# Inverse square roots by GpSimd's power with one Newton step, and a convolution's first tap on ScalarE, in a hybrid encoder layer

## The chip, the cores and the metric

The kernel runs on one core of a Trainium2 chip. The core has five engines, each with its own instruction queue worked off in order: TensorE (PE, with PEld for its weight loads), VectorE (DVE), ScalarE (ACT), GpSimd (POOL) and SyncE (SP, which here only issues DMAs). They meet through semaphores. The metric is the device time of one execution in microseconds; a kernel's time is the median of its runs.

## The reference

One layer of an encoder: 2048 tokens, 1024 channels, three head groups that read the same normalised input, an output projection, then a gated MLP with a causal depthwise convolution, and a last normalisation. Cut to what the change touches:

```python
def rmsnorm(x, g):
    r = lax.rsqrt(jnp.mean(xf * xf, axis=-1, keepdims=True) + EPS)
    return (xf * r * g).astype(x.dtype)

# x -> h = rmsnorm(x): input projection
#   A: S5 state-space layer + GLU
#   B: differential attention, 6 heads; o = rmsnorm(o, subln_g) per head
#   C: HGRN2 recurrence, 6 heads;       o = rmsnorm(o, norm_g) per head
# x = x + concat(A, B, C) @ w_out;      h = rmsnorm(x)

def conv_glu_ffn(h, w_up, w_gate, conv_w, conv_b, w_down):
    up = h @ w_up
    gate = h @ w_gate
    up = causal_depthwise_conv(up, conv_w, width=3) + conv_b
    return (jax.nn.gelu(up) * gate) @ w_down
# x = x + conv_glu_ffn(h); out = rmsnorm(x)
```

## The kernel before

All large products are float16 triples: each operand is split into a high half and a low half, and three products are summed (`three`, line 93). A split (`split`, line 51) is an ACT copy that makes the high half and a subtraction on DVE (lines 60 and 62) or POOL (line 58) that makes the low one. The feed-forward products are further cut by a seven-product scheme of sums of quarters: seven products per 128 channels, with their sums on DVE and POOL (`add`, line 1836; tiles `f_k`, `f_u`).

Stages, in the order of time of the profiled execution:

- 0 to 500 us: the input is normalised (`norm`, line 206) and projected, and head group A runs beside it.
- 500 to 1160 us: attention for the first eight query blocks (`phase_attn`) is woven with head group C (`phase_hgrn`). Per query block and head: scores on PE (tile `t_ps`, line 834), a biased copy with running maximum on DVE (`t_sc`, `t_mx`, line 838), the exponential on ACT (line 850), a join of the two maps on DVE (line 869), the split on ACT (line 892) and POOL (line 893), a transposing DMA, and the product with the values on PE (`t_po`, line 915).
- 1160 to 1300 us: the output projection of the first half of the tokens, its normalisation (`scaled`, line 1509) and the transposes that feed the MLP.
- 1300 to 1860 us: the up and gate products with their convolution for the first half (`activations`, `tile_of`: 22 channel tiles), woven with attention for the last eight query blocks.
- 1860 to 2190 us: the down product of the first half, the output projection of the second.
- 2190 to 2590 us: up and gate products of the second half; 2590 to 2794 us: its down product, with the last normalisation (`finish`, line 1593).

What is woven is decided by generators with weights, and a scheduler then sets each engine's queue by its own timeline of the whole program. So a changed instruction in one place can shift rows on every engine behind it.

`Ctx.rsqrt` (line 66) makes an inverse square root of a [128, n] tile v wholly on DVE: a shift (line 72) and an integer form (line 75) give a guess `y` (tile `rs_y`), then three Newton steps, each of lines 81, 86 and 87 (tile `rs_t`); for n = 1 line 79 makes -v/2 once and line 86 falls away. So 11 DVE instructions for n > 1 and 9 for n = 1. It is called 48 times:

| caller | tile v | n | calls |
|---|---|---|---|
| `norm` of the input | `a_v` | 4 | 4 |
| `fin` of head group C | `g_ss` | 8 | 12 |
| `norm` of an attention head | `t_e` | 8 | 12 |
| `scaled` | `o_v` | 4 | 4 |
| `finish` | `f_v` | 1 | 16 |

`conv` (line 1608) runs once per channel tile and token half, 44 times: the first tap (line 1609) scales `u` into `t0` (tile `f_t`) by a channel's weight, two further taps (line 1613) add to it, all three on DVE over 128x1024 float32. ACT's GELU (line 1884) reads the sum, then DVE multiplies it with the gate (line 1888).

Of the kernel before, what the change touches and what calls it, by code (L numbers as in the profile page):

```python
# [9 lines left out]
F32 = mybir.dt.float32  # L10
F16 = mybir.dt.float16
I32 = mybir.dt.int32
U8 = mybir.dt.uint8
AF = mybir.ActivationFunctionType
ALU = mybir.AluOpType
# [24 lines left out]
class Ctx:  # L40


    def __init__(self, tc, const):
        self.tc = tc
        self.nc = nc = tc.nc
        self.ident = const.tile([128, 128], F32, name="ident")
        make_identity(nc, self.ident)
        self.pairs = []
        self.pace = 1.0

# [15 lines left out]
    def rsqrt(self, pool, v, n, tag):  # L66

        nc = self.nc
        i = pool.tile([128, n], I32, tag=tag + "i", name="rs_i")
        y = pool.tile([128, n], F32, tag=tag + "y", name="rs_y")  # L70
        t = pool.tile([128, n], F32, tag=tag + "t", name="rs_t")
        nc.vector.tensor_scalar(
            out=i, in0=v.bitcast(I32), scalar1=1, scalar2=None, op0=ALU.logical_shift_right
        )
        nc.vector.tensor_scalar(
            out=y.bitcast(I32), in0=i, scalar1=-1.0, scalar2=float(0x5F3759DF), op0=ALU.mult, op1=ALU.add
        )
        if n == 1:
            nc.vector.tensor_scalar(out=i.bitcast(F32), in0=v, scalar1=-0.5, scalar2=None, op0=ALU.mult)
        for _ in range(3):  # L80
            nc.vector.scalar_tensor_tensor(
                out=t, in0=y, scalar=i.bitcast(F32)[:, 0:1] if n == 1 else -0.5, in1=y,
                op0=ALU.mult, op1=ALU.mult,
            )
            if n > 1:
                nc.vector.tensor_tensor(out=t, in0=t, in1=v, op=ALU.mult)
            nc.vector.scalar_tensor_tensor(
                out=y, in0=t, scalar=1.5, in1=y, op0=ALU.add, op1=ALU.mult
            )
        return y  # L90
# [1330 lines left out]
def phase_tail(K, x, Xd, Yd, Ad, w_out, norm_g, W, conv_w, conv_b, w_down, final_g, out, es,  # L1421
# [5 lines left out]
    tc, nc = K.tc, K.nc  # L1427
    V = nc.vector
# [15 lines left out]
    cw = cp.tile([128, 3, MF], F32, name="f_cw")  # L1444
# [161 lines left out]
            nc.sync.dma_start(out=out[0, r0:r0 + 128, cc], in_=r[:, cc])  # L1606

    def conv(u, t0, m, n):
        V.tensor_scalar(
            out=t0, in0=u[:, 0:n], scalar1=cw[:, 0, m:m + 1], scalar2=None, op0=ALU.mult  # L1610
        )
        for c in (1, 2):
            V.scalar_tensor_tensor(  # L1613
                out=t0, in0=u[:, c:n + c], scalar=cw[:, c, m:m + 1], in1=t0,
                op0=ALU.mult, op1=ALU.add,
            )
# [222 lines left out]
    def tile_of(hc, m, st, sm, wp, tp, pm, few, done, new):  # L1839
# [16 lines left out]
        def room(i, bufs=None):  # L1856
# [24 lines left out]
        nc.scalar.copy(halo[:, m, :], u[:, N:])  # L1881
        t0 = tp.tile([128, N], F32, tag="t0", bufs=few + 1, name="f_t0")
        conv(u, t0, m, N)
        nc.scalar.activation(
            out=t0, in_=t0, func=AF.Gelu_apprx_tanh, bias=cb[:, m:m + 1], scale=IWS
# [232 lines left out]
```

## Time and profile before

| what | before |
|---|---|
| median of 3 runs | 2815.44 us (2808.53 to 2818.59) |
| the profiled execution, its own time | 2795.69 us |
| its span | 2794.0 us |
| busy: PE, DVE, ACT, POOL | 2442.0, 2004.2, 1222.2, 1309.4 us |
| instructions on DVE, ACT, POOL | 3893, 2231, 1095 |
| mean granted TensorE clock | 0.93 |

Busy time is summed over the whole span, while the stages differ: an engine that is busy 72% of the span, as DVE is, can be the one that is waited for in some stages and of no account in others. A row of a group of instructions reads: source line, engine, operation, output tile, input tiles, shapes, count, busy time in us, mean duration in ns, then the idle time of that engine just ahead of these instructions and what ended it.

### The profile page before, as it was taken

The page shows a single profiled execution, that of the slowest core. Times are in us where ns is not written, and L with a number is a line of the kernel's source. Part 1 is how long each engine was busy: PE and PEld are TensorE (multiplying, and loading weights), DVE is VectorE, ACT ScalarE, POOL GpSimd, SP SyncE. Part 2 cuts the span into 40 slices and gives each one's busy share as a digit, 9 for nine tenths or more (in the row PEclk, how much of TensorE's full clock was granted, in tenths as well). Part 3 has the DMA queues.
Part 4 walks back from the last instruction along what each step waited for, and adds up shares of the span by engine and source line. Part 5 has one row for each costly group of instructions (what it writes and reads, how often), then busy time and mean ns, then how long its engine had stood idle before and what let it go on. Part 6 is the DMA issues. An engine that isn't in the chain of part 4 may idle for free. (4 is left out here: it accounts for less than half of the span.)

```text
span 2794.0 us, 42749 instructions
## 1 busy us (share of the span) xinstructions
PE 2442.0 (87%) x15438; PEld 1375.0 (49%) x15438; DVE 2004.2 (72%) x3893; ACT 1222.2 (44%) x2231; POOL 1309.4 (47%) x1095
## 2 busy tenths in 40 slices
PE   5998897989988888677998887859899999999998
PEld 3654546867766764243443333324344444444443
DVE  7466746789988897688779899975654855555575
ACT  5333344556645663565345555552234422222221
POOL 4788602334334432246666666631802344444180
PEclk8999998989989988788999999979999999999999
DMA  6675554555464656864455655587775655554733
GB/s 226 232 219 192 162 174 101 123 131 132 90 150 98 132 130 134 253 171 120 164 172 158 175 140 159 142 256 239 258 268 192 221 164 154 166 155 143 270 103 121
DMA packets 554533, 474.13 MB, mean 170 GB/s; under 512 B 276880, under 2 KB 432848, under 8 KB 553296
## 3 DMA queue, kind: packets, MB, share of 16 engines
q1 hardware_dynamic: 532144, 431.02, 54.1%
q10 hardware_dynamic: 22176, 40.38, 4.0%
q8 instruction: 121, 1.98, 0.3%
q14 instruction: 92, 0.75, 0.1%
HBM read 289.30 MB, written 127.93 MB: 149 GB/s over the span
## 5 line engine op out<-in xcount | busy, mean ns | idle before, releaser
L98 PE MATMUL f_pm<-f_q,f_w 128*128 128x512 f16 x3696 | 841.3, 387 | 37.9 <-DVE f_u L1837 21.7
L98 PEld LDWEIGHTS <-f_w 128*128 128x128 f16 x3696 | 363.7, 99 | 506.7 <-issue 90.4
L1772 PE MATMUL f_pd<-f_dw,f_da 128*128 128x512 f16 x1848 | 406.5, 383 | 11.7 <-DVE f_r L1750 10.4
L893 POOL TENSOR_TENSOR t_sc<-t_sc 128x1024 f16<-128x1024 f32 (+7 forms) x144 | 250.2, 1749 | 338.9 <-ACT t_sc L892 313.5
L1772 PEld LDWEIGHTS <-f_da 128*128 128x128 f16 x1848 | 181.8, 99 | 233.0 <-issue 18.5
L850 ACT ACTIVATE t_sc<-t_sc,t_nm 128x128 f32<-128x128 f32 (+7 forms) x192 | 229.1, 1195 | 99.1 <-DVE t_nm L845 91.7
L834 PE MATMUL t_ps<-t_k,t_q 96*128 96x512 f16 (+2 forms) x480 | 168.7, 377 | 99.0 <-DVE t_mx L838 86.6
L838 DVE CUSTOM_DVE_ANT_0 t_sc<-t_ps,t_base,t_mx 128x512 f32<-128x512 f32 (+3 forms) x288 | 185.1, 643 | 28.2 <-PE t_ps L834 21.5
L60 DVE TENSOR_TENSOR f_a<-f_t,f_a 128x512 f16<-128x512 f32 x132 | 148.1, 1129 | 46.1 <-ACT f_a L54 42.0
L98 PE MATMUL g_pq<-g_h,g_w 128*128 128x256 f16 x1152 | 158.6, 298 | 16.7 <-DVE g_sg L1162 10.6
L915 PE MATMUL t_po<-t_v,t_wt 128*128 128x64 f16 x2448 | 123.2, 201 | 56.4 <-DMA t_wt<-t_sc 48.7
L915 PEld LDWEIGHTS <-t_wt 128*128 128x128 f16 x2448 | 109.2, 104 | 123.1 <-DMA t_wt<-t_sc 67.0
L1837 POOL TENSOR_TENSOR f_t<-f_t,f_t 128x512 f32<-128x512 f32 x66 | 106.8, 1632 | 129.3 <-ACT f_a L54 108.3
L1487 PE MATMUL o_pm<-o_w,o_y 128*128 128x512 f16 x624 | 147.1, 394 | 19.9 <-DMA o_y<-Yd 14.1
L869 DVE SCALAR_TENSOR_TENSOR t_sc<-t_sc,t_a 128x1024 f32<-128x1024 f32 (+7 forms) x144 | 163.2, 1159 | 0.9
L1837 POOL TENSOR_TENSOR f_k<-f_k,f_k 128x512 f32<-128x512 f32 x88 | 124.7, 1417 | 73.2 <-ACT f_k L1869 68.3
L98 PE MATMUL g_pv<-g_w,g_h 128*128 128x256 f16 x1152 | 151.5, 288 | 8.0 <-ACT g_w L54 4.7
L62 DVE SCALAR_TENSOR_TENSOR f_dw<-f_db,f_dw 128x1536 f16<-128x1536 f32 (+1 forms) x36 | 104.1, 2910 | 73.8 <-ACT f_dw L54 73.7
L1837 POOL TENSOR_TENSOR f_db<-f_db 128x1536 f32<-128x1536 f32 (+1 forms) x32 | 128.2, 4044 | 60.6 <-DMA f_db<-in_w_down_dram 60.6
L892 ACT CAST t_sc<-t_sc 128x1024 f16<-128x1024 f32 (+7 forms) x144 | 112.1, 793 | 93.1 <-DVE t_sc L869 89.5
L54 ACT ACTIVATE f_w<-f_sum 128x512 f16<-128x512 f32 x110 | 69.2, 629 | 182.4 <-DVE f_sum L141 76.9
L54 ACT ACTIVATE f_a<-f_t 128x512 f16<-128x512 f32 x154 | 95.5, 628 | 114.5 <-POOL f_t L1837 56.6
(327 smaller groups left out, 4534.8 us busy)
## 6 DMA issues: line engine op xcount, KB each, us to landing
f_w<-Wd SPq DMA_DIRECT2D x231, 256.0 KB, 3.0
Wd<-f_w SPq DMA_DIRECT2D x154, 256.0 KB, 2.1
Ad<-f_a ACTq DMA_DIRECT2D x154, 256.0 KB, 2.8
f_da<-Ad SPq DMA_DIRECT2D x42, 768.0 KB, 4.4
g_h<-Hd SPq DMA_DIRECT2D x24, 1024.0 KB, 7.0
f_db<-in_w_down_dram SPq DMA_DIRECT2D x24, 768.0 KB, 10.5
o_wst<-in_w_out_dram SPq DMA_DIRECT2D x32, 512.0 KB, 5.4
o_y<-Yd SPq DMA_DIRECT2D x52, 256.0 KB, 4.7
```

Source lines behind the costliest of these rows:

```text
L54: nc.scalar.activation(out=hi, in_=src, func=AF.Copy, scale=scale)
L60: nc.vector.tensor_tensor(out=lo, in0=src, in1=hi, op=ALU.subtract)
L98: nc.tensor.matmul(out=out, lhsT=lhs(a, k), rhs=rhs(b, k), start=(n == 0), stop=(n == 3 * nk - 1))
L834: nc.tensor.matmul(out=ps[:, 0:k1 - k0], lhsT=qt[:, c, 128 * (i % 4):128 * (i % 4) + 128], rhs=H.k[:, c, k0:k1], start=True, stop=True,)
L838: V.tensor_tensor_reduce(out=sc[c][:, k0:k1], in0=ps[:, 0:k1 - k0], in1=bs[:, k0:k1], scale=1.0, scalar=-3e38 if j == 0 else mx[:, c, j - ...
L850: nc.scalar.activation(out=sc[c][:, 0:L], in_=sc[c][:, 0:L], func=AF.Exp, scale=SLOPES[h], bias=nm[:, c:c + 1], accum_out=H.la[:, c, n_:n_ ...
L869: V.scalar_tensor_tensor(out=sc[0][:, k0:k1], in0=sc[1][:, k0:k1], scalar=a[:, 1:2], in1=sc[0][:, k0:k1], op0=ALU.mult, op1=ALU.add,)
L893: nc.gpsimd.tensor_tensor(out=hl[:, LM + k0:LM + k1], in0=sc[0][:, k0:k1], in1=hl[:, k0:k1], op=ALU.subtract,)
L915: nc.tensor.matmul(out=po, lhsT=wt[:, w, b, :], rhs=vt[:, b, 64 * v:64 * v + 64], start=(b == 0 and w + v == 0), stop=(b == i and w == 1),)
L1487: nc.tensor.matmul(out=ps[t], lhsT=y[:, k, a, 128 * t:128 * t + 128], rhs=w[:, b, k, :], start=(q == qs[0] and i == 0), stop=(q == qs[-1] ...
L1772: nc.tensor.matmul(out=ps[t], lhsT=a[:, q, x, tk], rhs=w[:, y, q, :], start=(first and q + x + y == 0), stop=(last and q == n - 1 and y == 1),
L1837: eng.tensor_tensor(out=o, in0=a, in1=b, op=op)
```

## The change

Two edits. `rsqrt` starts from GpSimd's `tensor_tensor` with the power operation: y = v to the power of a constant -0.5, read with stride 0 from a [128, 1] tile `mhalf`; one Newton step on DVE follows. The guess, its tile `rs_i` and two of the three Newton steps go. For n = 1 the one step is written as three instructions. In `conv` the first tap becomes an ACT copy with the weight as its per-partition scale.

```diff
+        self.mhalf = const.tile([128, 1], F32, name="mhalf")
+        nc.gpsimd.memset(self.mhalf, -0.5)
...
     def rsqrt(self, pool, v, n, tag):
-        i = pool.tile([128, n], I32, tag=tag + "i", name="rs_i")
         y = pool.tile([128, n], F32, tag=tag + "y", name="rs_y")
         t = pool.tile([128, n], F32, tag=tag + "t", name="rs_t")
-        nc.vector.tensor_scalar(
-            out=i, in0=v.bitcast(I32), scalar1=1, scalar2=None, op0=ALU.logical_shift_right
-        )
-        nc.vector.tensor_scalar(
-            out=y.bitcast(I32), in0=i, scalar1=-1.0, scalar2=float(0x5F3759DF), op0=ALU.mult, op1=ALU.add
-        )
-        if n == 1:
-            nc.vector.tensor_scalar(out=i.bitcast(F32), in0=v, scalar1=-0.5, scalar2=None, op0=ALU.mult)
-        for _ in range(3):
-            nc.vector.scalar_tensor_tensor(
-                out=t, in0=y, scalar=i.bitcast(F32)[:, 0:1] if n == 1 else -0.5, in1=y,
-                op0=ALU.mult, op1=ALU.mult,
-            )
-            if n > 1:
-                nc.vector.tensor_tensor(out=t, in0=t, in1=v, op=ALU.mult)
+        nc.gpsimd.tensor_tensor(
+            out=y, in0=v, in1=self.mhalf.to_broadcast([128, n]), op=ALU.pow
+        )
+        nc.vector.scalar_tensor_tensor(
+            out=t, in0=y, scalar=v[:, 0:1] if n == 1 else -0.5, in1=y, op0=ALU.mult, op1=ALU.mult
+        )
+        if n == 1:
+            nc.vector.tensor_scalar(
+                out=t, in0=t, scalar1=-0.5, scalar2=1.5, op0=ALU.mult, op1=ALU.add
+            )
+            nc.vector.tensor_tensor(out=y, in0=y, in1=t, op=ALU.mult)
+        else:
+            nc.vector.tensor_tensor(out=t, in0=t, in1=v, op=ALU.mult)
             nc.vector.scalar_tensor_tensor(
                 out=y, in0=t, scalar=1.5, in1=y, op0=ALU.add, op1=ALU.mult
             )
...
     def conv(u, t0, m, n):
-        V.tensor_scalar(
-            out=t0, in0=u[:, 0:n], scalar1=cw[:, 0, m:m + 1], scalar2=None, op0=ALU.mult
-        )
+        nc.scalar.activation(out=t0, in_=u[:, 0:n], func=AF.Copy, scale=cw[:, 0, m:m + 1])
```

The change alters no data movement in the source; the scheduler orders the queues anew. Lines behind the edits move up by one to three, so line 87 of before is line 86 now, and 1613 is 1610.

Where it moves instructions, first on DVE, at the first inverse root of head group C (`g_ss` is v, `g_d` a decay factor of that group, `t_sc` and `t_mx` the scores of attention). Before:

```order
L72 TENSOR_SCALAR rs_i<-g_ss 128x8
L845 SCALAR_TENSOR_TENSOR t_nm<-t_mx,t_lk 128x2
L75 TENSOR_SCALAR rs_y<-rs_i 128x8
L81 SCALAR_TENSOR_TENSOR rs_t<-rs_y 128x8
L1232 TENSOR_TENSOR g_d<-g_d,g_k 128x32x8
L86 TENSOR_TENSOR rs_t<-rs_t,g_ss 128x8
L1233 TENSOR_TENSOR g_d<-g_d,g_q 128x32x8
L87 SCALAR_TENSOR_TENSOR rs_y<-rs_t,rs_y 128x8
L81 SCALAR_TENSOR_TENSOR rs_t<-rs_y 128x8
L929 RECIPROCAL t_e_5730<-t_la 128x8
L86 TENSOR_TENSOR rs_t<-rs_t,g_ss 128x8
```

And now, from the instruction that finishes v (line 1341):

```order
L1341 TENSOR_SCALAR g_ss<-g_ss 128x8
L837 ISA t_sc,t_mx<-t_ps,t_base,t_mx 128x512
L837 ISA t_mx 128x1
L1231 TENSOR_TENSOR g_d<-g_d,g_k 128x32x8
L1232 TENSOR_TENSOR g_d<-g_d,g_q 128x32x8
L76 SCALAR_TENSOR_TENSOR rs_t<-rs_y 128x8
L85 TENSOR_TENSOR rs_t<-rs_t,g_ss 128x8
L86 SCALAR_TENSOR_TENSOR rs_y<-rs_t,rs_y 128x8
```

The guess and two steps are gone, and between v and the step that is left stand four rows of other work. The step waits for POOL, whose queue at the same place now holds the power (`g_y` is the group's output, `t_sc` the low half of an attention row that line 892 makes):

```order
L1227 TENSOR_TENSOR g_d<-g_b 128x32x8
L1346 TENSOR_TENSOR g_y<-g_y,g_sg 128x512
L892 TENSOR_TENSOR t_sc<-t_sc 128x896
L73 TENSOR_TENSOR rs_y<-g_ss,mhalf 128x8
L1181 TENSOR_SCALAR g_k<-g_x,g_f_3709,g_f_3711 128x512
L1266 TENSOR_TENSOR g_d<-g_b 128x512
```

The power stands behind a product and a low half that wait for ACT, and ahead of head group C's next rows. Over all 48 calls there are 0 to 18 DVE instructions between v and the Newton step, 10 at the median of the 25 that lie between 500 and 1860 us.

Second, the convolution of one channel tile (`f_t_15484` before, `f_t_15270` now) while the up products run beside attention. On DVE before:

```order
L1837 TENSOR_TENSOR f_u<-f_pm_15437,f_u 128x512
L1609 TENSOR_SCALAR f_t_15484<-f_u,f_cw 128x1024
L62 SCALAR_TENSOR_TENSOR f_w<-f_wst,f_w 128x512
L1837 TENSOR_TENSOR f_k_15284<-f_pm_15466,f_k_15284 128x512
L1613 SCALAR_TENSOR_TENSOR f_t_15484<-f_u,f_cw,f_t_15484 128x1024 x2
L62 SCALAR_TENSOR_TENSOR f_w<-f_sum,f_w 128x512
```

And on ACT now:

```order
L1878 COPY f_halo<-f_u 128x2
L56 ACTIVATE f_w<-f_sum 128x512
L56 ACTIVATE f_w<-f_wst 128x512
L1608 ACTIVATE f_t_15270<-f_u,f_cw 128x1024
L1861 COPY f_k_15286<-f_pm_15301 128x512
L56 ACTIVATE f_w<-f_sum 128x512
L1881 ACTIVATE f_t_15270<-f_t_15270,f_cb 128x1024
```

The first tap left DVE's queue; on ACT it stands two rows ahead of the GELU of the same tile, with a copy out of PSUM and a weight's high half between them, and the other two taps follow it on DVE.

## The prediction

> **What bounds the kernel now.** I first read the page's head and its slices (the span in 40 equal parts, each digit an engine's busy share in tenths), to find where the engines' roles change.
>
> ```profile
> span 2794.0 us, 42749 instructions
> PE   5998897989988888677998887859899999999998
> DVE  7466746789988897688779899975654855555575
> ```
>
> From slice 32 on PE is full and DVE half busy; in slices 7 to 14 and 19 to 25 both stand at eight or nine tenths. The busy times of each engine stage by stage (start and end, length, then PE, PEld, DVE, ACT and POOL) put numbers on it, and the chain that ended last says what holds the end.
>
> ```profile
> 500.00:1160.00 660.00, 563.68 (x5454) 424.22 (x5454) 561.21 (x1547) 377.03 (x798) 254.42 (x212) 0.88 0.58 130
> 1300.00:1860.00 560.00, 460.11 (x2582) 212.44 (x2581) 480.54 (x712) 282.88 (x467) 358.42 (x231) 0.93 0.56 166
> 2190.00:2590.00 400.00, 399.99 (x1850) 181.08 (x1849) 231.06 (x306) 114.11 (x210) 182.00 (x139) 1.00 0.53 164
> ...
> PE 28%; DVE 7%; DMA 4%; issue 3%; ACT 2%; POOL 1%; SPq 1%; DVEq 0%; ACTq 0%; POOLq 0%
> ...
> 2210.63 375.71 PE f_pm L98 x1740
> 2586.34 199.44 PE f_pd L1772 x924
> ```
>
> The last 600 us are one run of matmuls on PE: whatever DVE saves there is worth nothing but at the very end. The chain is followed back only to about 1490; its DVE part is 7% of 2794, some 196 us, and lies between 1490 and 2188 (28% of that stretch). So the change can pay in two stages: 500 to 1160, where PE idles 660 - 564 = 96 us and DVE is 85% busy, and 1300 to 1860, where PE idles 100 us and DVE is 86% busy. What ended PE's idle time (total us, times, longest), first of 1300 to 1860, then of 500 to 1160:
>
> ```profile
> PE t_ps L834 <- DVE t_mx L838: 47.5, 33, 5.9
> PE f_pm L98 <- DVE f_u L1837: 21.7, 9, 5.9
> ...
> PE t_po L915 <- DMA t_wt<-t_sc: 29.1, 20, 4.4
> PE t_ps L834 <- DVE t_mx L838: 20.3, 37, 1.8
> ...
> PE o_pm L1487 <- DVE o_w L62: 1.5, 1, 1.5
> ```
>
> In the later stage DVE ends at least 69 of 100 us, in the earlier 39.5 of 96 (seven DVE rows, of which the first and the last are shown), with the transposing DMA ahead of them.
>
> **The change part by part.** *Stage 500 to 1160.* Twenty inverse roots are made here. Their rows in that window:
>
> ```profile
> L81 DVE SCALAR_TENSOR_TENSOR rs_t<-rs_y 128x8 f32<-128x8 f32 x60 | 14.5, 241 | 0.8
> L87 DVE SCALAR_TENSOR_TENSOR rs_y<-rs_t,rs_y 128x8 f32<-128x8 f32 x60 | 12.1, 201 | 0.9
> L86 DVE TENSOR_TENSOR rs_t<-rs_t,t_e 128x8 f32<-128x8 f32 x24 | 8.2, 341 | 0.3
> L86 DVE TENSOR_TENSOR rs_t<-rs_t,g_ss 128x8 f32<-128x8 f32 x36 | 7.1, 197 | 0.6
> L72 DVE TENSOR_SCALAR rs_i<-g_ss 128x8 int32<-128x8 int32 x12 | 6.6, 552 | 0.0
> L75 DVE TENSOR_SCALAR rs_y<-rs_i 128x8 int32<-128x8 int32 x20 | 6.2, 309 | 0.1
> L72 DVE TENSOR_SCALAR rs_i<-t_e 128x8 int32<-128x8 int32 x8 | 1.7, 209 | 0.0
> ...
> L87 DVE SCALAR_TENSOR_TENSOR rs_y<-rs_t,rs_y 128x8 f32<-128x8 f32 (+2 forms) x144 | 28.5, 201 | 2.0
> ```
>
> Together 56.4 us. Of lines 81, 86 and 87 (41.9 us) one third stays, 14.0 us, so 42.4 us leave by busy time. But line 72 means 552 ns on one tile and 209 on the other for the same shape: single ones are held up by something else, and such a hold falls on whatever stands next. Without the holds, at the 0.16 us at which most of them run (the smaller means above lie at 0.2), 160 instructions are 26 us. I take the middle, 34. How much of it shortens the stage lies between 0.2 (the scores' share of PE's idle time, 20.3 of 96) and 0.4 (that of all seven DVE rows); at a third it is **-11 us**.
>
> *Stage 1300 to 1860.* Twenty-two first taps and two inverse roots:
>
> ```profile
> L1609 DVE TENSOR_SCALAR f_t<-f_u,f_cw 128x1024 f32<-128x1024 f32 x22 | 19.8, 900 | 0.4
> L81 DVE SCALAR_TENSOR_TENSOR rs_t<-rs_y 128x8 f32<-128x8 f32 x6 | 4.1, 687 | 0.1
> L86 DVE TENSOR_TENSOR rs_t<-rs_t,t_e 128x8 f32<-128x8 f32 x6 | 3.8, 634 | 0.0
> L87 DVE SCALAR_TENSOR_TENSOR rs_y<-rs_t,rs_y 128x8 f32<-128x8 f32 x6 | 1.5, 246 | 0.0
> ```
>
> 19.8 leave with the taps; of the 9.4 us of Newton steps two thirds, 6.3, and the guess, some 1.6 (four at about 0.4): 27.7 us. The share that counts lies between 28% (DVE on the chain) and 69% (PE's idle time that DVE ends). I take 40%, nearer the chain, which is the direct reading: **-11 us**.
>
> *ACT's new work.* ACT already scales 128x1024 float32 by a per-partition factor:
>
> ```profile
> L1523 ACT ACTIVATE f_q<-o_r,rs_y x4: 1132/1138/1147, 1163.8 to 2105.2; 128x1024 f32<-128x1024 f32 x4
> ```
>
> 22 x 1.14 = 25 us more on an engine that was 283 of 560 us busy. ACT holds 2% of the span on the chain, 56 us of the 698 us between 1490 and 2188, or 8%: **+2 us**. Behind the tap in its queue stand the copies out of PSUM, the GELU and attention's exponentials; if they all wait for it, the full 25 us is the upper end. In the other half's 22 tiles PE's unbroken run hides both sides. A tap takes 1.14 us there instead of 0.90, so one tile's chain grows by about a quarter of a us.
>
> The Trainium skill speaks against this edit (ScalarE: Activation LUTs, Rules for kernel authors): a multiplication belongs on VectorE and not on ScalarE. The rows agree on the single instruction, 1.14 against 0.90 us. By that rule alone the edit would cost 22 x 0.24 = 5 us on the tiles' own chains instead of giving, and the sum would come out near -4 us; it leaves out that the freed engine is the one waited for, which the 69 us above say.
>
> *1160 to 1300.* Two normalisations (`scaled`) stand with nothing to cover them. First and last DVE step of the second, then the input's first normalisation (line 222 writes v), then the last one of `finish`:
>
> ```profile
> 1228.76 0.16 DVE L1512 SCALAR_TENSOR_TENSOR o_v<-o_ss 128x4 f32<-128x4 f32 x1
> 1234.27 0.16 DVE L87 SCALAR_TENSOR_TENSOR rs_y<-rs_t,rs_y 128x4 f32<-128x4 f32 x1
> ...
> 10.70 0.17 DVE L222 TENSOR_SCALAR a_v<-a_ss 128x4 f32<-128x4 f32 x1
> 12.09 1.23 DVE L62 SCALAR_TENSOR_TENSOR a_wu<-a_wst,a_wu 128x1024 f16<-128x1024 f32 x1 [0.22 <-ACT a_wu L54]
> 15.02 0.16 DVE L87 SCALAR_TENSOR_TENSOR rs_y<-rs_t,rs_y 128x4 f32<-128x4 f32 x1
> ...
> 2787.35 0.16 DVE L1596 SCALAR_TENSOR_TENSOR f_v<-f_ss 128x1 f32<-128x1 f32 x1 [0.85 <-ACT f_sq L1588]
> 2789.26 0.16 DVE L87 SCALAR_TENSOR_TENSOR rs_y<-rs_t,rs_y 128x1 f32<-128x1 f32 x1
> ```
>
> The price of the power is in no row. The nearest are POOL's elementwise products of the same size, and the farthest its longest elementwise row:
>
> ```profile
> L580 POOL TENSOR_TENSOR s_tb<-s_sn,s_col 128x8 f32<-128x8 f32 x4 | 1.7, 424 | 0.0
> L1837 POOL TENSOR_TENSOR f_db<-f_db 128x1536 f32<-128x1536 f32 (+1 forms) x32 | 128.2, 4044 | 60.6 <-DMA f_db<-in_w_down_dram 60.6
> ```
>
> So 0.42 to 4.0 us; I take 0.5, from the row of its own shape. With 0.1 us for each of two hand-overs and three steps 0.2 us apart, a root takes about 1.3 us bare, against 11 x 0.2 = 2.2 (9 x 0.21 = 1.9 at the end). `scaled` stretched to 5.5 us at 1228 since other rows stood between its steps; fewer steps mean fewer such rows: **-2 us** for both. At the start the split of line 62 still ends at 13.3, then come three steps: scaled rows begin at about 14.0 instead of 15.2, **-1 us**. The end: **-0.6 us**; at 4.0 us for the power it would be +3.
>
> A sentence of the Trainium skill has another price (GPSIMD Engine Reference, Instruction dispatch): the first call of freshly loaded code costs about 6 us more, unseen. No run here shows it; by it the first power would land near 17 us and the sum would come out near -13.
>
> *The new waits.* The Newton step waits on POOL, and behind it DVE's whole queue, so the scores and joins of attention. POOL works in order and itself waits much (500 to 1160; below it how DVE has fared where POOL feeds it, 1190 to 1860):
>
> ```profile
> POOL t_sc L893 <- ACT t_sc L892: 216.2, 36, 18.6
> ...
> DVE t_sc L838 <- POOL t_sc L893: 4.5, 4, 1.9
> ...
> DVE f_u L1837 <- POOL f_u L1837: 11.2, 7, 2.6
> ```
>
> The order leaves 10 DVE instructions at the median between v and the step, 10 x 561/1547 = 3.6 us of cover. Where POOL feeds `f_u`, DVE waited 7 times in 22 tiles, 1.6 us each. A third of the 25 roots between 500 and 1860 at 1.6 us is 13 us, of which about a third counts: **+4 us**.
>
> Sum: -11 - 11 + 2 - 2 - 1 - 0.6 + 4 = about **-20 us**. Against the profiled execution's own 2795.7 that is 2776. The median of the runs shown is 2815.4, 0.7% above it, so there I forecast **2795 us**.
>
> **The rivals.** *The wait takes the place of the work (slower).* Place: DVE's queue at the 25 roots between 500 and 1860, each time with attention's scores behind it. If a power takes 4.0 us and stands behind one low half of line 893 (1.7 us), it lands 5.9 us after v, 2.3 past the cover; 25 x 2.3 = 58 us of DVE standing still. Without the +4 the rest of the sum is -24. At 40% the stall just eats it; where nothing else runs, it counts in full, +34. In between, at 70%, +17: 2832 us. It decides from about 6 us between v and the finished power. For it: POOL's 36 long waits for ACT, 18.6 us at most. Against: POOL's low halves held DVE up for only 4.5 us there before, and the order gives each root room.
>
> *PE and its DMA set the pace (no change).* If in 500 to 1160 the transposes (29 us of PE's waits) come late next and ACT's 25 us stand in the way in 1300 to 1860, only the bare parts and a few us stay: -5, 2810 us. For it: PE at 85% in both.
>
> *DVE alone sets both stages (much faster).* Then 0.8 of 42 + 28 count, -56, and the bare parts: 2756 us. Against: the chain gives DVE 28%.
>
> That the change does not do what it says is excluded by the order: 48 powers on POOL, and the guess and two of three steps gone from DVE.
>
> **How the numbers follow.** Forecast (-9 to -35 us) 0.50, much faster 0.12, no change 0.20, slower 0.18. About 0.3%, 8 us, is what a measurement of this kernel can tell from no change. So faster by more than that 0.62, within 0.20, slower 0.18. The range takes the much faster case in and the slower one at its middle price: 2754 to 2832; beyond lie the slower case's full price and a power far dearer than any row, about 0.15.
>
> **What would show it.** Right: DVE's busy time falls by 80 to 100 us, ACT's rises by 50; PE's waits on `t_mx` and `f_u` in the two stages shrink by some 20 us together; the stage 2190 to 2794 keeps its length. Wrong: DVE waits at the first Newton step with POOL as releaser, over 40 us in sum; a power of over 3 us; a stage 500 to 1160 that keeps its 660 us with DVE less busy; GELU rows that come later because ACT is behind.

## The result

| kernel | median of its runs | ratio to the kernel before |
|---|---|---|
| before, beside it | 2811.99 us (2807.10 to 2818.59, 4 runs) | 1 |
| changed | 2769.23 us (2766.96 to 2772.72, 4 runs) | 0.9858 [0.9835, 0.9882] |

The change makes the kernel 42.8 us faster, where 20 us were forecast; the time lies inside the range and the sign is as forecast; the size is not, and the gain does not sit where the forecast put it. The profiled execution of the changed kernel took 2772.72 us, against 2795.69 us of the one before: between these two the gain is 23.0 us.

The page of the changed kernel, in the order in which that of before was read: head, slices, stages (start and end, length, then PE, PEld, DVE, ACT and POOL, granted clock, DMA share), chain.

```profile
span 2771.0 us, 42468 instructions
PE   5998889988988888868987988769999999999998
DVE  7567746888878987688778998963654755555475
...
500.00:1160.00 660.00, 564.97 (x5378) 420.28 (x5378) 542.27 (x1376) 383.46 (x798) 284.42 (x229) 0.87 0.61 138
1300.00:1860.00 560.00, 469.93 (x2641) 217.88 (x2639) 462.97 (x673) 308.76 (x492) 343.79 (x223) 0.91 0.59 173
2190.00:2590.00 400.00, 400.00 (x1855) 181.38 (x1854) 210.97 (x239) 140.42 (x227) 178.85 (x139) 1.00 0.53 160
...
PE 36%; DVE 15%; DMA 9%; issue 8%; ACT 6%; POOL 5%; SPq 1%; ACTq 0%; DVEq 0%; POOLq 0%
```

The roles are the same: PE full at the end, PE and DVE at eight or nine tenths in the two woven stages. DVE lost 19 us of busy time between 500 and 1160 and 18 between 1300 and 1860, ACT and POOL gained. The shares of the chain can't be set beside those of before, since it is followed back much further here (they add up to 80% of the span instead of 46%). What ended PE's idle time, first of 1300 to 1860, then of 500 to 1160 (total us, times, longest):

```profile
PE t_ps L833 <- DVE t_mx L837: 44.4, 30, 4.4
PE f_pm L97 <- DVE f_u L1834: 22.8, 8, 8.6
...
PE t_po L914 <- DMA t_wt<-t_sc: 22.9, 23, 3.3
PE t_ps L833 <- DVE t_mx L837: 22.0, 28, 3.7
```

Here is the first surprise. The waits on DVE that the forecast wanted 20 us shorter (47.5 + 21.7 and 20.3 us before) are the same within 3 us or so. They are the same, too, when the windows follow the work, which stands up to 33 us earlier now (between the events named next: 61.6 + 21.7 and 25.0 us before, 53.4 + 24.9 and 30.7 now). To see where the gain sits, the span is cut at four events on PE: the first product of the input's projection (`a_p` from `a_h`), the first up product (`f_pm`), the first down product (`f_pd`), and the start of the last one. In the views by tile (count, min/median/max ns, first and last start) these are, first of before, then of the changed kernel:

```profile
L98 PE MATMUL a_p<-a_h,a_w x576: 378/379/635, 117.1 to 392.6; 128*128 128x512 f16 x192
L98 PE MATMUL f_pm<-f_q,f_w x3696: 376/379/635, 1253.1 to 2586.0; 128*128 128x512 f16 x195
L1772 PE MATMUL f_pd<-f_dw,f_da x1848: 376/379/632, 1861.9 to 2785.4; 128*128 128x512 f16 x185
...
L97 PE MATMUL a_p<-a_h,a_w x576: 379/379/634, 106.6 to 381.6; 128*128 128x512 f16 x192
L97 PE MATMUL f_pm<-f_q,f_w x3696: 376/379/634, 1221.5 to 2563.6; 128*128 128x512 f16 x195
L1769 PE MATMUL f_pd<-f_dw,f_da x1848: 376/379/634, 1829.1 to 2763.0; 128*128 128x512 f16 x185
```

| stretch | before | changed | gain |
|---|---|---|---|
| start to first `a_p` | 117.1 | 106.6 | 10.5 |
| to first `f_pm` (rest of group A, attention woven with group C, first output projection) | 1136.0 | 1114.9 | 21.1 |
| to first `f_pd` (up products woven with attention) | 608.8 | 607.6 | 1.2 |
| to last `f_pd` | 923.5 | 933.9 | -10.4 |

So it came from the start, where -1 was forecast, and from the first woven stage; the stage of the taps gave nothing, and the last third gave 10 us back. The cut at the first `f_pm` does not part the same work in both, though. The two middle stretches, first of before, then of the changed kernel (start and end, length, busy time of PE, PEld, DVE, ACT and POOL with their instructions, granted clock):

```profile
117.10:1253.10 1136.00, 969.77 (x7933) 673.82 (x7931) 858.98 (x2123) 573.35 (x1169) 493.10 (x586) 0.90 0.60 152
1253.10:1861.90 608.80, 493.50 (x2757) 227.39 (x2757) 524.24 (x783) 313.58 (x522) 383.68 (x247) 0.91 0.54 159
...
106.60:1221.50 1114.90, 960.93 (x7869) 671.35 (x7867) 834.79 (x1916) 569.16 (x1159) 535.23 (x617) 0.90 0.62 154
1221.50:1829.10 607.60, 497.15 (x2822) 231.28 (x2821) 517.80 (x768) 339.93 (x552) 389.82 (x251) 0.90 0.56 161
```

Sixty-four of attention's products, 6 to 8 us of PE's time, stand ahead of the first `f_pm` before and behind it now. PE's idle time, which this does not touch, fell from 166.2 to 154.0 us in the first of the two stretches and from 115.3 to 110.5 in the second.

What the new operations cost. The power on POOL (min/median/max ns), DVE's wait for it over the whole span, the tap on ACT, and a small attention row of DVE, before and now:

```profile
L73 POOL TENSOR_TENSOR rs_y<-f_v,mhalf x16: 537/548/1672, 2028.6 to 2765.2; 128x1 f32<-128x1 f32 x16
L73 POOL TENSOR_TENSOR rs_y<-g_ss,mhalf x12: 1632/1638/2604, 494.7 to 1082.5; 128x8 f32<-128x8 f32 x12
L73 POOL TENSOR_TENSOR rs_y<-a_v,mhalf x4: 1027/1044/1202, 11.0 to 71.4; 128x4 f32<-128x4 f32 x4
...
DVE rs_t L76 <- POOL rs_y L73: 6.5, 11, 1.1
...
L1608 ACT ACTIVATE f_t<-f_u,f_cw 128x1024 f32<-128x1024 f32 x44 | 50.5, 1148 | 127.4 <-DVE f_u L1834 122.3 <-POOL t_sc L892 5.1
...
L845 DVE SCALAR_TENSOR_TENSOR t_nm<-t_mx,t_lk 128x2 f32<-128x2 f32 x96 | 28.0, 293 | 0.6
...
L844 DVE SCALAR_TENSOR_TENSOR t_nm<-t_mx,t_lk 128x2 f32<-128x2 f32 x96 | 40.1, 420 | 0.6
```

The power is three times as dear as priced at eight columns (1.64 us, not 0.5), but its wait is 6.5 us in all. And by the groups of rows, the 496 root instructions of 120.6 us became 144 of 38.0, and 44 taps of 37.6 us left: 120 us of busy time. Yet DVE's total fell by 62.6 us only, from 2004.2 to 1941.6. The other 57.6 us came back in rows that nobody touched, such as the last one shown: the same 96 instructions take 12 us more. The last section shows what holds such rows up.

### The profile page after: what moved, and what is told of

It is laid out like the page before. It is cut to its first block, busy times and chain, and to the rows that moved or that the text cites. A ratio compares the mean times of both kernels' runs of the same rounds, so it can differ in the third digit from the quotient of the medians.

```text
span 2771.0 us, 42468 instructions
## 1 busy us (share of the span) xinstructions
PE 2437.1 (88%) x15438; PEld 1374.1 (50%) x15438; DVE 1941.6 (70%) x3497; ACT 1269.5 (46%) x2273; POOL 1362.6 (49%) x1144
## 4 chain that ended last, share of the span: by engine, by line
PE 36%; DVE 15%; DMA 9%; issue 8%; ACT 6%; POOL 5%; SPq 1%; ACTq 0%; DVEq 0%; POOLq 0%
PE f_pm L97 15%; PE f_pd L1769 10%; PE o_pm L1486 3%; DVE t_sc L837 3%; DMA t_wt<-t_sc 2%; DVE t_sc L868 2%; ACT t_sc L849 2%; DMA f_dst<-in_w_down_dram 2%; PE g_pq L97 2%; DMA o_y<-Yd 1%; PE g_pv L97 1%; POOL t_sc L892 1%; DVE f_w L64 1%; DVE f_t L1610 1%; DVE f_a L62 1%
## 5 line engine op out<-in xcount | busy, mean ns | idle before, releaser
L97 PE MATMUL f_pm<-f_q,f_w 128*128 128x512 f16 x3696 | 844.3, 388 | 43.3 <-DVE f_u L1834 24.9
L62 DVE TENSOR_TENSOR f_a<-f_t,f_a 128x512 f16<-128x512 f32 x132 | 158.3, 1219 | 50.1 <-ACT f_a L56 49.6
L97 PE MATMUL g_pv<-g_w,g_h 128*128 128x256 f16 x1152 | 157.1, 294 | 9.1 <-ACT g_w L56 8.1
L1486 PE MATMUL o_pm<-o_w,o_y 128*128 128x512 f16 x624 | 144.1, 389 | 20.8 <-DMA o_y<-Yd 10.4
L1610 DVE SCALAR_TENSOR_TENSOR f_t<-f_u,f_cw,f_t 128x1024 f32<-128x1024 f32 x88 | 125.8, 1429 | 32.6 <-ACT f_t L1608 32.3
L837 DVE CUSTOM_DVE_ANT_0 t_sc<-t_ps,t_base 128x512 f32<-128x512 f32 (+2 forms) x192 | 120.8, 633 | 37.7 <-PE t_ps L833 19.1
```

Of the source, the lines that this page charges most:

```text
L62: nc.vector.tensor_tensor(out=lo, in0=src, in1=hi, op=ALU.subtract)
L97: nc.tensor.matmul(out=out, lhsT=lhs(a, k), rhs=rhs(b, k), start=(n == 0), stop=(n == 3 * nk - 1))
L837: V.tensor_tensor_reduce(out=sc[c][:, k0:k1], in0=ps[:, 0:k1 - k0], in1=bs[:, k0:k1], scale=1.0, scalar=-3e38 if j == 0 else mx[:, c, j - ...
L1486: nc.tensor.matmul(out=ps[t], lhsT=y[:, k, a, 128 * t:128 * t + 128], rhs=w[:, b, k, :], start=(q == qs[0] and i == 0), stop=(q == qs[-1] ...
L1610: V.scalar_tensor_tensor(out=t0, in0=u[:, c:n + c], scalar=cw[:, c, m:m + 1], in1=t0, op0=ALU.mult, op1=ALU.add,)
```

## The experiments

Two theories stood at first: W, the gain is the work that DVE lost; O, a good part of it is the new order in which the scheduler put the woven stages once durations had changed. Each run was compared with runs of the kernel before on the same chip. That kernel's 90 runs beside the experiments have a median of 2805.5 us and reach from 2791.7 to 2819.5.

### One part alone

`e1_rsqrt_only`: the new root, the tap as before.

```diff
-        nc.scalar.activation(out=t0, in_=u[:, 0:n], func=AF.Copy, scale=cw[:, 0, m:m + 1])
+        V.tensor_scalar(
+            out=t0, in0=u[:, 0:n], scalar1=cw[:, 0, m:m + 1], scalar2=None, op0=ALU.mult
+        )
```

> The inverse roots as in the changed kernel, the first tap back on VectorE. Theory W (the gain is DVE work taken out of stretches where DVE is full, almost all of it by the inverse roots: the first f_pm product starts 31.6 us earlier in the changed kernel's trace, the stretch with the taps is only 1.2 us shorter): 36 to 43 us faster than before, 2769 to 2776 us against 2812. Theory C (the taps carry the 9 us net that the prediction gave them): 34 us faster at most, 2778 us or more. Theory O (the scheduler's new order of the queues, not the work, moves the time): anything, also slower than before.

`e2_conv_only`: the kernel before with the changed line of `conv`, the root as before.

> Only the first tap on ScalarE, inverse roots as before. Theory W: 0 to 5 us faster than before (2807 to 2812 us), since the taps' stretch hardly shortened in the changed kernel and the second half's taps lie beside PE's unbroken run. Theory C: 9 us faster (2803 us). Theory O: anything within 20 us of before.

`e5_start_only`: the kernel before with the new root in the four `a_v` normalisations of the input alone. `e6_all_but_start`: the changed kernel with the old root there.

```diff
-                r = K.rsqrt(sp, v, 4, "rs")
+                r = K.rsqrt(sp, v, 4, "rs", old=False)
```

> The new inverse root only in the four normalisations of the input (a_v), all else as before. Theory W: these four cost 15 us of DVE busy time in the first 120 us, where DVE is full from 20 to 80 us; the input projection starts 10.5 us earlier in the changed kernel. So 8 to 11 us faster than before, 2801 to 2804 us. The prediction's own step (only the first of the four is on the path): 1 us, 2811 us. Theory O: the later stages move by more than that either way.

> The changed kernel with the old inverse root in the four normalisations of the input. Theory W: it lacks those 8 to 11 us and keeps the rest, 2777 to 2782 us. The prediction's own step: it lacks 1 us, 2770 us. Theory O: its parts and those of the run with the start only don't add up to the whole, by more than 10 us.

| kernel | median us | ratio to before |
|---|---|---|
| e1: roots alone | 2770.94 | 0.9879 [0.9859, 0.9899] |
| e2: taps alone | 2799.62 | 0.9982 [0.9964, 0.9999] |
| e5: the four roots of the start alone | 2801.38 | 0.9985 [0.9972, 0.9999] |
| e6: everything but those four | 2809.61 | 1.0009 [0.9994, 1.0024] |

The roots carry nearly all of it, the taps about 5 us (0 to 10 by the interval). But the parts don't add: by the ratios the start gives 4 us, all the rest gives nothing, and both together 40. The stretch from the first `a_p` to the first `f_pm` shows why: 1136.0 us before, 1151.2 in e5, 1147.7 in e6, 1114.9 with both. In e5 the work in it is that of before, instruction for instruction apart from the order, and it takes 15 us longer. Some of the 15 is not the order: the profiled execution of before was 10 us shorter than that kernel's median, and that of e5 was not (2801.23 us).

### The order by itself

The weave's weights are numbers in `LW`. A little change of the fourth one leaves every instruction as it is and moves rows on all queues.

```diff
-LW = [6.0, 0.44, 5.0, 2.5, 0.62, 1.0]
+LW = [6.0, 0.44, 5.0, 2.48, 0.62, 1.0]
```

The same with 2.52, 2.45 and 2.55, each for the kernel before and for the changed one: five pairs with the one at 2.5.

> The kernel before with one number of the weave's weights changed (the fourth of LW, 2.5 to 2.48): the same instructions on every engine, put into another order in the stage where attention is woven with head group C (500 to 1160 us) and behind it. Theory W (the 43 us between the kernels are the work taken off VectorE): 2807 us, within 5 either way, since no work is taken off. Theory O (a good part of the 43 us is the order in which the weave happened to put the work once its durations changed): this variant lies 10 us or more from the kernel before, in either direction, and the stretch from the last product of the input projection's first rows to the first feed-forward product carries the difference.

> The changed kernel with the same one number changed (2.5 to 2.48). Theory W: 2770 us, within 5. Theory O: 10 us or more away from the changed kernel, and the distance to the variant of the kernel before with the same number is another than 43 us; if the work alone is worth what was forecast, 20 us.

> The kernel before with the fourth of LW at 2.52 in place of 2.5: the same instructions, another order. Theory W: 2807 us within 5. Theory O: 10 us or more from it, and not at the place of the 2.48 variant.

> The changed kernel with the fourth of LW at 2.52. Theory W: 2770 us within 5. Theory O: 10 us or more from it. The mean of the distances between the pairs with equal weights (2.48, 2.5, 2.52) is then the estimate of what the work is worth: 43 us by theory W, 20 us by theory O with the forecast's size.

> A fourth pair of orders: the kernel before with the fourth of LW at 2.45 in place of 2.5, all instructions the same. So far the distances between the pairs were 36 to 43 us (2.5), 28 us (2.48) and 13 us (2.52), so that neither theory W alone (43 everywhere) nor the order alone (nothing on the mean) holds. Mixed theory: the work is worth the mean, some 25 us, and an order moves either kernel by up to 10 us to each side; then this variant lies between 2785 and 2815 us. Theory W by itself would want 2805 within 5.

> The changed kernel with the fourth of LW at 2.45. Mixed theory: between 2765 and 2790 us, and 10 to 40 us under the variant of the kernel before with the same number. Theory W: 2770 us within 5. A distance under 10 us would speak for the order as the main cause.

> The kernel before with the fourth of LW at 2.55: a fifth pair of orders. Mixed theory (work worth some 21 us, the order up to 10 to each side of either kernel): between 2785 and 2810 us.

> The changed kernel with the fourth of LW at 2.55. Mixed theory: between 2765 and 2787 us, and 5 to 40 under the kernel before with the same number. The work worth 36 to 43 by itself: 2765, and more than 30 under it.

| weight | before, us | its ratio | changed, us | its ratio | distance of the ratios |
|---|---|---|---|---|---|
| 2.45 | 2786.39 | 0.9933 [0.9918, 0.9948] | 2778.16 | 0.9907 [0.9885, 0.9929] | 0.0026 |
| 2.48 | 2809.49 | 1.0012 [0.9998, 1.0026] | 2781.75 | 0.9916 [0.9884, 0.9947] | 0.0096 |
| 2.5 | 2811.99 | 1 | 2769.23 | 0.9858 [0.9835, 0.9882] | 0.0142 |
| 2.52 | 2787.61 | 0.9940 [0.9918, 0.9962] | 2774.23 | 0.9884 [0.9857, 0.9911] | 0.0056 |
| 2.55 | 2829.21 | 1.0097 [1.0078, 1.0116] | 2791.52 | 0.9953 [0.9936, 0.9970] | 0.0144 |

All ratios are to the kernel before at 2.5. Theory W alone falls: equal work differs by up to 1.6%, 46 us, among the orders of the kernel before, and by 0.95% among those of the changed one. Theory O alone falls too: at every weight the changed kernel is ahead, though at 2.45 by 7 us only, which the intervals do not set apart from nothing. The bands of 10 us that the last two expectations gave an order were too narrow: both variants at 2.55 lie above theirs. The mean distance is 0.0093, 26 us; with five pairs and their scatter (0.0052) its 95% interval reaches from 8 to 44 us. The changed kernel at 2.5 is the fastest of all that ran.

### Taps and powers under other orders

> The new roots alone (first tap on VectorE) with the fourth of LW at 2.48. At 2.5 the move of the taps gave 2 us on top of the roots. If the taps are worth the 9 us that were forecast for them (-11 with +2 on ScalarE) and the order hid it at 2.5, then this is some 9 us slower than the changed kernel at 2.48 (2781.8), 2791 us. If they are worth nothing, it is within the scatter of the orders around 2775 us and the three distances (2.48, 2.5, 2.52) have no common sign.

> The new roots alone with the fourth of LW at 2.52. Taps worth 9 us: 2783 us (the changed kernel at 2.52 takes 2774.2). Taps worth nothing: 2774 us, within 8 for the order.

> The kernel before with the first tap on ScalarE alone, fourth of LW at 2.52. Taps worth 9 us: 2779 us (the kernel before at 2.52 takes 2787.6). Taps worth next to nothing: 2788 us, within the 8 us by which orders differ.

`e7_one_step` is the kernel before with the changed line of `conv` and with one Newton step in place of three, on VectorE, and no power; `e7_w248` and `e7_w252` the same at two other weights.

```diff
-        for _ in range(3):
+        for _ in range(1):
```

> The bit-level guess with one Newton step in place of three, wholly on VectorE, and the first tap on ScalarE; two Newton steps of each inverse root are left out, so the values are less exact. VectorE does two instructions more per root than in the changed kernel (one more for n = 1) and nothing is handed to GpSimd. If the hand-overs cost the 4 us that were forecast, or less, this lands within the scatter of the orders around the changed kernels, 2769 to 2782 us. If waits for GpSimd's power ate a good part of the gain, it lands clearly under all of them, below 2762 us.

> The variant with one Newton step on VectorE alone (two steps left out), first tap on ScalarE, with the fourth of LW at 2.48. If 2808 us was its order: 2775 to 2795 us, near the changed kernel at 2.48 (2781.8). If less work on VectorE is worth nothing by itself and only the hand-over to GpSimd pays: about 2805 us again, at both weights.

> The same with the fourth of LW at 2.52. Its order: 2770 to 2792 us (the changed kernel at 2.52 takes 2774.2). Otherwise 2800 us or more.

| kernel | 2.48 | 2.5 | 2.52 |
|---|---|---|---|
| before | 1.0012 | 1 | 0.9940 |
| e1: roots alone | 0.9899 [0.9883, 0.9914] | 0.9879 | 0.9929 [0.9912, 0.9947] |
| e2: taps alone | | 0.9982 | 0.9955 [0.9936, 0.9975] |
| changed | 0.9916 | 0.9858 | 0.9884 |
| e7: one step, no power, taps moved | 0.9960 [0.9941, 0.9978] | 1.0015 [0.9999, 1.0030] | 0.9899 [0.9866, 0.9932] |

The tap's move is worth -0.0018 and +0.0015 without the new roots (e2 to before), and +0.0017, -0.0021 and -0.0045 with them (changed to e1): no common sign (at 2.52 with the new roots the 9 us were there, and without them not), 3 us on the mean instead of the 9 that were forecast. Five values that scatter so leave an interval from 12 us faster to 6 slower, so the 9 are not excluded. The roots alone (e1 to before) gave 0.0113, 0.0121 and 0.0011: they carry the gain at two weights and not at the third. Where the time went that DVE gained by the taps' move stands in its waits between the first `f_pm` and the first `f_pd`; first of before, then of the changed kernel, of e2 and of e1:

```profile
DVE t_a L862 <- ACT t_sc L850: 15.9, 13, 3.5
...
DVE t_a L861 <- ACT t_sc L849: 26.9, 19, 2.8
DVE f_t L1610 <- ACT f_t L1608: 5.6, 9, 1.2
...
DVE t_a L862 <- ACT t_sc L850: 25.4, 16, 2.7
DVE f_t L1611 <- ACT f_t L1609: 5.9, 9, 1.2
...
DVE t_a L861 <- ACT t_sc L849: 12.5, 13, 2.1
```

`t_a` is the join of the two attention maps, which waits for ACT's exponential. With the tap on ACT this wait was 20.1 to 27.8 us in the seven traces of the changed kernel and of e2 (mean 24.4), with the tap on DVE 9.9 to 18.8 in the eight of before and of e1 (mean 14.3). It is 10 us longer, and 5 more go to the second tap, which now waits for the first. Of the 19.8 us that DVE lost in this stage it waits 15 away. (In the runs left out of these means it was 20.5 in e6, 15.9 in e5 and 18.1 to 23.7 in the three of e7, named below.)

A longer wait has two readings: the exponentials come later, or DVE comes to the join sooner. They can be told apart by setting each `t_nm` (the row on DVE that the exponentials wait for) beside its exponentials and its join, by order; 18 to 22 such sets lie in the stage. In the seven traces with the tap on ACT the join starts 4.17 to 4.59 us after `t_nm` on the mean of a trace, in the eight others 4.31 to 4.86: it does not come later. The exponentials start later by 4.6 us over the whole stage (their delays behind `t_nm` add up to 16.7 us against 12.1), and taps run between a `t_nm` and the end of its exponentials for 1.7 us at most in a trace. So half or less of the longer wait is ACT being late; the rest is DVE arriving early, with less work ahead of the join.

e7 frees 256 of the 352 root instructions that the change frees, and all taps, without the power. On the mean it lies between before and changed, 7 us ahead of the one and 20 behind the other; at 2.5 it is not ahead of before at all. At 2808 us it missed what either theory had expected of it, and at 2.48 it lies above the band given for its order. Set beside e2, which differs from it by the two Newton steps alone, it is 0.0056 (16 us) faster at 2.52 and 0.0033 (9 us) slower at 2.5. So fewer rows on DVE can pay without the power, and can also not pay; whether its distance to the changed kernel (0.0044, 0.0157 and 0.0015 at 2.48, 2.5 and 2.52) is the two instructions more per root (five against three, for n = 1 as well), the power or the order stays open.

## Why the prediction was right or wrong

The forecast gain of 20 us is less than half of the 42.8 that came, and the two parts of the shortfall have different causes. Between the two profiled executions the kernel gained 23.0 us, 3 more than the sum said; there the terms failed one by one and made up for each other, which is luck: the start, "-1", and the way to the first `f_pm`, "-11 - 2", gave 10.5 and 21.1 us, the taps' stage, "-11 + 2", gave 1.2, and the last third, priced at nothing, cost 10.4. The other 19.8 us lie between the profiled executions and the medians: that of before was 16.3 us under the median of its runs, that of the changed kernel 3.5 over its own. The step that failed there is the lift by 0.7%, which took both to lie equally far under their medians.

**What bounds the kernel: right, with one wrong inference.** The last stage kept its length (2190 to 2590 is all PE, before and now). But the 500 us ahead of the woven stages got one term, of 1 us, and 10.5 us of the gain lie there, all before the first `a_p`.

**The start, "-1 us": wrong, the mis-sized term.** Only the first of the four `a_v` roots was priced, and by the time of its last three steps. The fourth, on DVE before, with the POOL row that is in its way and ACT's and POOL's users of y (start, duration):

```profile
72.31 0.16 DVE L222 TENSOR_SCALAR a_v<-a_ss 128x4 f32<-128x4 f32 x1
...
85.38 5.63 POOL L58 TENSOR_TENSOR a_w<-a_wst,a_w 128x1024 f16<-128x1024 f32 x2
86.24 2.10 DVE L81 SCALAR_TENSOR_TENSOR rs_t<-rs_y 128x4 f32<-128x4 f32 x1
88.94 2.09 DVE L86 TENSOR_TENSOR rs_t<-rs_t,a_v 128x4 f32<-128x4 f32 x1
91.96 0.15 DVE L87 SCALAR_TENSOR_TENSOR rs_y<-rs_t,rs_y 128x4 f32<-128x4 f32 x1
92.15 2.19 ACT L229 ACTIVATE a_x<-a_x,rs_y 128x1024 f32<-128x1024 f32 x2 [4.90 <-DVE rs_y L87]
```

And in the changed kernel:

```profile
71.14 0.16 DVE L221 TENSOR_SCALAR a_v<-a_ss 128x4 f32<-128x4 f32 x1
71.38 1.04 POOL L73 TENSOR_TENSOR rs_y<-a_v,mhalf 128x4 f32<-128x4 f32 x1 [4.45 <-DVE a_v L221]
74.54 0.16 DVE L76 SCALAR_TENSOR_TENSOR rs_t<-rs_y 128x4 f32<-128x4 f32 x1
77.02 0.16 DVE L86 SCALAR_TENSOR_TENSOR rs_y<-rs_t,rs_y 128x4 f32<-128x4 f32 x1
77.21 2.19 ACT L228 ACTIVATE a_x<-a_x,rs_y 128x1024 f32<-128x1024 f32 x2 [1.88 <-DVE rs_y L86]
```

Each of the eleven steps queued behind other rows of DVE, two of them were held for 2.1 us, and y came 20 us after v; now it comes after 6. The scaled rows that wait for it stand 15 us earlier. The forecast counted busy time; the price of a chain on a full engine is the number of its steps times what stands between them. In e7, with five steps, y comes 6.5 us after v (68.9 to 75.4). In all 8 traces with the old root there, the last two scaled rows of ACT start at 92.2 to 95.2 us, in all 9 with the power at 77.2 to 78.6. How much of the 15 us PE sees is another matter: the first `a_p` stands at 116.1 to 119.6 us in the ones, at 106.6 to 114.5 in the others (on the mean over the five pairs 6.2 us earlier), and what decides between 107 and 114 is the granted clock, the figure behind POOL's in these rows of the changed kernel at 2.5 and at 2.48:

```profile
80.00:100.00 20.00, 18.63 (x161) 16.54 (x160) 16.42 (x27) 9.04 (x15) 17.23 (x13) 0.95 0.64 217
...
80.00:100.00 20.00, 18.63 (x129) 16.23 (x127) 16.01 (x26) 8.59 (x15) 17.23 (x13) 0.76 0.54 186
```

The rows up to there stand in the same order in both; PE is equally busy and does 161 matmuls at a clock of 0.95 and 129 at 0.76. Over 80 to 115 us the clock was 0.95 to 0.97 in the four traces that start `a_p` by 107.6 us, 0.90 in the one that does at 110.2, and 0.76 in the four that do at 113.9 or later. Why it differs stays open.

**500 to 1160, "-11", with 1160 to 1300, "-2": right in kind on the mean of the pairs, too small at this weight, its size not settled.** Over the five pairs the stretch from the first `a_p` to the first `f_pm` became shorter by 21.1, 31.0, 0.8, 15.9 and 47.7 us (weights 2.5, 2.48, 2.52, 2.45, 2.55), 23 on the mean. Before's own five lie 36 us apart (1128.9 to 1164.7), the changed kernel's 13 (1114.9 to 1128.1). PE's idle time in it fell by 13.7 us on the mean of the pairs (by 25.0 at most, and at 2.52 it rose by 4.7), of which 10.9 are waits that DVE ended; this is about what the two terms said. The other 9.5 us are busy time of PE, mostly attention's products that stand behind the first `f_pm` now. The step that failed is to take one trace's waits for what the work costs: at 2.5 all the waits that DVE ended stayed (80.0 and 81.4 us), while those for the transposing DMAs, which were thought to come "late next", fell from 36.2 to 23.2 us though no DMA changed (29.1 to 22.9 in the window shown). The two `scaled` roots behaved as priced: the second took 3.9 us instead of 5.7, the first 0.2 more.

**1300 to 1860, "-11", and ACT, "+2": wrong.** Over the five pairs the stretch became longer by 2 us on the mean. It holds 37 more of attention's products on the mean, but PE's idle time in it did not fall either: 110.5 us before and 110.0 on the mean of the pairs. The taps left as counted, and DVE waited most of the freed time away, 10 us more for exponentials (some 5 of them because these start later) and 5 for the tap itself. What failed is the 40% of the freed time that was to reach PE, a choice between the 28% and the 69% of one trace. ACT's "+2" was small too: ACT's share of the chain was read as a price for more work on ACT, and it only says how late ACT was with the work that it had. By the taps alone PE's idle time in it changed by -6.2 and 0.0 us (e2 to before) and by -7.0, +6.7 and -11.8 (changed to e1), -3.7 on the mean, so a part of the forecast may be there; the scatter does not let it be told. The Trainium skill's rule (ScalarE: Activation LUTs, Rules for kernel authors), by which a multiplication belongs on VectorE, gave -4 us for the whole change (worked out again, -11 - 2 - 1 - 0.6 + 4 + 5 is about -6); the mean of the pairs, -26 us, does not support it. On the taps by themselves the measured -3 us lie between its +5 and the forecast's -9.

**The end, "-0.6": right.** From v to y at the last root 2.1 us before (2787.35 to 2789.42) and 1.4 now (2764.99 to 2766.42).

**The last third, unpriced.** From the first to the last `f_pd` all five pairs became longer, by 4.6 to 10.4 us, 7.6 on the mean, with the same up, down and output products in it. (At 2.48, 2.52 and 2.45 also 8 to 37 more of attention's products.) At 2.5 PE's waits there make 31 us instead of 24; the new ones are a wait for ACT's copy into `f_k` (3.9 us), one for a down weight's DMA (3.6) and one for attention's last rows (2.5). The taps are not needed for it, since e1, with the tap on DVE, takes 933.7 us there and the changed kernel 933.9. It may be that what ran ahead earlier meets the weights here; this was not tested.

**The new waits, "+4": right, rather less.** 6.5 us in 11 waits, though the price of the power was off by three: the 10 instructions between v and the step cover 1.64 us easily. The slower rival needed 6 us between v and the finished power; at the 25 roots between 500 and 1860 it was 1.1 to 5.6 us, 1.9 at the median. The Trainium skill's 6 us for the first call of freshly loaded code (GPSIMD Engine Reference, Instruction dispatch) did not show: the first power ran from 11.01 us for 1.03, and its Newton step stood at 13.29, behind the split as forecast. (The -13 that the forecast gave for this case is worked out wrongly: a power landing near 17 us would put the scaled rows about 3 us later than before instead of 1 earlier, and the sum near -16.)

**Against which time.** The forecast for the profiled execution was 2776 us, and 2772.7 came. It was then lifted by 0.7% because the profile of before lay 0.7% under the median of its runs. The profile of before was one of its shortest executions (2795.7 against a median of 2805.5 over 90), and that of the changed kernel is not (2772.7, the slowest of its four). Against 2805.5 the change gains 36 us, not 43.

**The signs.** ACT's busy time rose by 47 us, where 50 were named. DVE's fell by 62.6, where 80 to 100 were, and the waits on `t_mx` and `f_u` did not shrink. The end was to keep its length; from the first `f_pd` on it became longer.

Taken together: the sum of the five pairs' stretches is -6.2 - 23.3 + 2.2 + 7.6 = -19.7 us by the traces (and 0.6 more behind the last `f_pd`), -26 us by the medians, and the forecast's -20 is within the interval of the medians, 8 to 44. Of the 42.8 us, 6.5 are that the four runs of before lie above its usual median; the 10 that are left beyond the mean are put down to the order at 2.5, which the scatter of the pairs allows and no run shows by itself. The composition was wrong all the same: nearly half of the forecast sat in the stage of the taps, where PE's idle time did not fall, and almost none of it on the start.

## What to carry to other kernels

A chain of small dependent instructions on a busy engine costs its number of steps times the queue between them, not its busy time; look for it where a whole stage waits for its end, at the start above all. Time taken off an engine is not a gain until someone who waits for that engine gets it: look at what the freed engine waits for next, as here for the exponentials, and set what it waits for beside its own input before calling it late. Where a scheduler lays out the whole program anew, time a change under several neutral orders before its size is believed: here one order of the same work differed from another by more than the change is worth.

## What was not expected of the hardware

**POOL holds small DVE rows up, its power does not.** DVE rows that read and write at most eight columns were set beside POOL's rows by start and duration, in the two traces of the result. Before, 670 of them touch no POOL row and take 0.28 us at most; of 187 that touch one, 61 take over 0.5 us, 2.31 at most. In the changed kernel 365 touch none (0.28 at most). Of the 146 that touch a POOL row other than a power 62 take over 0.5 us, but of the 33 beside a power none takes over 0.27. A Newton step beside a weight's sum and the next row beside a low half, then a join beside a power, all of the changed kernel:

```profile
1500.31 1.26 POOL L140 TENSOR_TENSOR f_sum<-f_wst 128x512 f32<-128x512 f32 x1 [0.63 <-DVE rs_t L85]
1500.34 1.25 DVE L86 SCALAR_TENSOR_TENSOR rs_y<-rs_t,rs_y 128x8 f32<-128x8 f32 x1
1501.53 2.75 POOL L892 TENSOR_TENSOR t_sc<-t_sc 128x1024 f16<-128x1024 f32 x2
1501.63 2.04 DVE L935 TENSOR_TENSOR t_e<-t_e,rs_y 128x8 f32<-128x8 f32 x1
...
521.55 1.64 POOL L73 TENSOR_TENSOR rs_y<-t_e,mhalf 128x8 f32<-128x8 f32 x1 [6.29 <-DVE t_a L861]
521.63 0.62 DVE L868 SCALAR_TENSOR_TENSOR t_sc<-t_sc,t_a 128x384 f32<-128x384 f32 x1
```

A held row ends when the POOL row does: 59 of the 61 and all 62 end within 0.03 us behind a POOL row's end (the low half shown at 1501.53 is two rows, the first of which ends at 1503.65). As many rows over 0.5 us are left (61 and 62) though 352 small ones are gone: the hold falls on whatever stands next. That is how a part of the 120 us came back; of the `t_nm` rows shown above 15 were held before and 28 are now. The Trainium skill says something near it (SBUF — State Buffer, Who interferes with whom): a DVE instruction with two inputs in SBUF contends with a GpSimd instruction that reads SBUF, and the ports they share are an exclusive lock. The trace agrees for 46 of the 61 held rows, which have two inputs, and for reciprocals, which have one: 34 beside POOL before, none over 0.20 us. It does not agree for the power, which reads SBUF as well: 18 rows with two inputs lay beside one and took 0.22 us at most. Two more things do not follow from that sentence: the other 15 held rows are `TENSOR_SCALAR`, with one input, and of 19 products of 128x256 in head group A that lay wholly inside a POOL row before, 18 took their usual 0.42 us.

**The power goes by columns.** 0.55, 1.04 and 1.64 us for 1, 4 and 8 columns, some 0.16 us for each further one.

**The time of an execution goes with its granted clock.** Of the 90 runs of the kernel before, the 28 with a mean clock of 0.924 or less took 2809 us on the mean, the 21 with 0.928 or more 2801. The same order holds on each of the five chips that ran it. The correlation is -0.67, so the clock goes with not quite half of the scatter.
